# Tile bases on multiples of 256 bytes, side b's filling work held closer to its place, and one addition of the closing norm moved to VectorE

## The chip, the cores and the metric

The kernel runs on one core of one Trainium2 chip. The metric is the device time of one launch in microseconds (us), the median of several runs. Engines are named as in the profile: PE is TensorE (matrix products), PEld its weight loads, DVE is VectorE, ACT ScalarE, POOL GpSimd, SP the engine that issues the DMAs.

## The reference, cut to what matters

One decoder layer on 1024 tokens of width 1024. A layer norm with a modulation from `c` gives `u`; one wide projection of `u` feeds two attention branches and two gates; a last product and a second norm close the layer.

```python
u = _layer_norm(x) * (1.0 + scale) + shift
(q_a, kv_cmp, kv_sel, kv_win, g_nsa, z_a, q_b, kv_b, z_b, g_merge) = _split_columns(u @ w_in)
# branch a: 8 heads; compressed keys, 8 selected blocks of 64 keys, a window of 512
o_a = gts0 * o_cmp + gts1 * o_sel + gts2 * o_win
y_a = o_a * silu(z_a)
# branch b: 8 heads, a window of 128 with a sink logit per head
y_b = _banded_attention(q_b, k_b, v_b, 128, sinks) * silu(z_b)
merged = sigmoid(gm_a) * (y_a @ w_up_a) + sigmoid(gm_b) * (y_b @ w_up_b)
out = merged @ w_out
x = _layer_norm(2 ** 0.25 * x + gate * out) * ln_g + ln_b
```

## The kernel before, in words

Every large product is made of three, to keep float32's precision: an operand is split into a high part (H) and a rest (L), both read as 32-bit "fp32r", and `H*h + H*l + L*h` is summed in PSUM. `load_w` (L239) and `load_w2` (L251) bring a block of weights in by DMA, cut it on ACT (the high part) and on POOL or DVE (the rest), and put both into one tile `whl`.

The stages, in order of time. **Start** (0 to some 140 us): `x` is normed and transposed into `uH` and `uL`, and the first columns of `w_in` are projected. **Attention** (to some 725 us): 32 units, one for each side (a, b), head group and tile of 128 tokens. A unit has three steps: `C` (L742) turns its queries and, on side a, does the compressed branch; `M` (L826) finds each row's maximum; then for each tile of 128 keys `score` (L892) makes two products 512 wide (keys against `qa`, then `qb`), DVE and ACT make `e`, ACT `ph`, POOL `pl`, and `weigh` (L915) multiplies both by the values in 12 short products. **Merge** (to some 850 us): products of `yH`, `yL` with `w_up`. **Close** (to the end): the product with `w_out` in two halves of 512 columns (weights in the pools `wo0` and `wo1`, 8 tiles of tokens each), then `residual` and `norm` (L1424, L1432) for each tile.

Between the attention's products stands *filling* work that depends on nothing there: query projections 256 columns wide (`q_chunk`), and 24 blocks of the gates (`gm_block`, 48 products of 512 columns each), 20 of them inside the attention and 4 after it. `Att.run` deals it out in small steps while it writes the attention down, and a step may not be ordered ahead of an anchor, the last product of an earlier `weigh`:

```python
with L.tc.issue_after(anchors[max(0, len(anchors) - ANCH)]):   # L976, ANCH = 9
    d = fill.step()
```

Within such bounds a scheduler sets the order of each engine's instructions when the program is built; on the chip each engine runs its list in order. Tiles come from pools that lay them one behind another in each partition, so that a tile's first byte depends on the sizes of those before it.

`norm` takes mean and variance of a tile (`mv`, DVE), lets POOL add eps and raise to -0.5 (`rstd`, two POOL instructions at L541 and L542, each on one number per partition), and scales on DVE in two passes, L1441 (needs only `mv`) and L1442 (needs `rstd`).

Of the kernel before, what the change touches and what calls it, by code (L numbers as in the profile page):

```python
# [7 lines left out]
F32 = mybir.dt.float32  # L8
F32R = mybir.dt.float32r
BF = mybir.dt.bfloat16  # L10
F16 = mybir.dt.float16
I32 = mybir.dt.int32
AF = mybir.ActivationFunctionType
OP = mybir.AluOpType
# [4 lines left out]
D = 1024  # L19
S = 1024  # L20
NT = 8
# [4 lines left out]
LN_EPS = 1e-5  # L26
# [7 lines left out]
PARTS = 4  # L34
TRB = (2, 3, 4, 5)
MS, PJ = (2, 3, 4), (6, 7)
ANCH = 9
WARM2 = 1
ADA0 = 3
W0AT = 7  # L40
# [3 lines left out]
TPOOL, TCUT = 0, (256, 256)  # L44
MROW = 1
KEEP = 4
CW = 20
M0 = 0
TAB = 2
# [27 lines left out]
VW = 129  # L77
# [20 lines left out]
class Layer:  # L98
# [32 lines left out]
    def identities(self):  # L131
        nc = self.nc
        ones = self.ones = self.su.tile([128, 128], F32, name="ones")
        nc.gpsimd.memset(ones, 1.0)
        self.idf = self.c.tile([128, 128], F32, name="idf")
        nc.gpsimd.affine_select(self.idf, ones, pattern=[[1, 128]], compare_op=OP.is_equal, fill=0.0, base=0,
                                channel_multiplier=-1)
        self.mhalf = self.c.tile([128, 1], F32, name="mhalf")
        nc.gpsimd.memset(self.mhalf, -0.5)
        self.onec = self.c.tile([128, 1], F32, name="onec")  # L140
        nc.gpsimd.memset(self.onec, 1.0)
        self.poff = self.c.tile([128, 1], F32, name="poff")
        nc.gpsimd.memset(self.poff, POFF)

    def consts(self):
# [93 lines left out]
    def load_w(self, src, k, n, rawp, wp, eng, **place):  # L239

        nc = self.nc
        raw = rawp.tile([128, max(n, 512) if rawp is self.rawp else n], F32, name="raw", tag="raw")[:, :n]
        self.rows_in = nc.sync.dma_start(raw, src(k)).ins
        hl = wp.tile([128, 2, n], F32R, name="whl", **(place or {"tag": "w"}))
        h, l = hl[:, 0, :], hl[:, 1, :]
        self.cast = nc.scalar.copy(h, raw).ins  # L246
        low = eng.tensor_tensor(l, raw, h.bitcast(F32), op=OP.subtract).ins  # L247
        self.low = [self.cast, low, self.low[1]]
        return h, l
# [86 lines left out]
    def start(self):  # L336
        nc, I = self.nc, self.I
        su, c = self.su, self.c
        x = I["x"].rearrange("a (t p) d -> (a t) p d", p=128)
        xt = []  # L340
        wa = I["w_ada"].rearrange("l (k p) c -> (l p) k c", p=128)
        wt, w = {}, {}
# [31 lines left out]
        ps, wps = self.bank(7), self.bank(6)  # L374
# [12 lines left out]
        pf = su.tile([8, 128], F32, name="pos_f")  # L387
        nc.vector.tensor_copy(pf, pi)
        nc.tensor.transpose(ps[:, 24:32], pf, self.idf[:8, :8])
        self.ccol = c.tile([128, 8], F32, name="ccol")  # L390
        bcol = su.tile([128, 16], F32, name="bcol")
        self.pos = su.tile([128, 8], F32, name="pos")
        with self.tc.high_priority(HP):
# [59 lines left out]
        for t in range(NT):  # L453
# [4 lines left out]
            nm, rstd, nb = ln[t]  # L458
# [4 lines left out]
            for hf in range(2):  # L463
                p = trs[t >= 4].tile([128, 4, 128])
# [126 lines left out]
    def new_kv(self, ps, br, vp):  # L591

        self.K[br] = [p.tile([128, 2, 1024], F32R, name=f"K{br}{g}") for g, p in enumerate(ps)]
        self.V[br] = [p.tile([128, NT, VW], F16, name=f"V{br}{g}") for g, p in enumerate(ps)]
        self.new_v(br, vp)

    def new_v(self, br, vp):
# [113 lines left out]
class Att:  # L711


    def __init__(self, L, q, work):

        self.L, self.q, self.w = L, q, work
        self.ms, self.st, self.av = Banks(L, MS), Banks(L, ST), Banks(L, (5,))
        nc = L.nc
        self.nc = nc
        self.U = {}  # L720
        self.qbt = []
        for i in range(2):
            q = work.tile([128, 4, 128], F32R, name=f"qbt{i}")
            nc.gpsimd.tensor_copy(q.rearrange("p h d -> p (h d)"), L.mk[:, 128:129].to_broadcast([128, 512]))
            self.qbt.append(q)
        self.p0 = work.tile([128, 68], F32, name="p0")
        nc.gpsimd.memset(self.p0, 0.0)
        self.n, self.last = 0, []
        self.off = [True, True]
# [9 lines left out]
    def C(self, u):  # L739
        L, nc, w = self.L, self.nc, self.w  # L740
        side, g, qt = u
# [7 lines left out]
                                                       op=OP.subtract)  # L749
# [15 lines left out]
        t = w.tile([128, 4, 64], F32, name="cs", tag="cs")  # L765
        nc.vector.tensor_tensor(t, sc[:, :, 1, :], L.vis[:, qt, None, :].to_broadcast([128, 4, 64]), op=OP.add)
        nc.vector.tensor_tensor(t, t, sc[:, :, 0, :], op=OP.add)
        sm = w.tile([128, 4, 4], F32, name="csm", tag="csm", bufs=2)
        nc.vector.tensor_reduce(sm[:, 0], t, axis=AX.X, op=OP.max)
        (nc.gpsimd if CM else nc.vector).tensor_tensor(t, t, sm[:, 0, :, None].to_broadcast([128, 4, 64]), op=OP.subtract)  # L770
        e = t
# [12 lines left out]
        if qt >= 4:  # L784
            nc.vector.tensor_reduce(self.p0[:, 1:64], pc[:, :, 0:63].rearrange("p h c -> p c h"), axis=AX.X, op=OP.add)
            im = w.tile([128, 4, 16], F32, name="imp", tag="imp")
            nc.vector.tensor_reduce(im[:, 0], self.p0[:, 0:64].rearrange("p (j i) -> p j i", i=4), axis=AX.X, op=OP.add)
            nc.gpsimd.tensor_tensor(im[:, 0], im[:, 0], rawap(self.p0, 4, [[4, 16]]), op=OP.add)
            nc.gpsimd.tensor_tensor(im[:, 1], im[:, 0], L.forced[:, qt], op=OP.add)
            m8 = w.tile([128, 8], F32, name="m8", tag="m8")  # L790
            nc.vector.max(m8, im[:, 1])
            nc.vector.match_replace(im[:, 2], m8, im[:, 1], -3e38)
            sel = st["sel"] = w.tile([128, 16], F32, name="sel", tag="sel", bufs=3)
            nc.vector.tensor_scalar(sel, im[:, 2], -2e38, NEG, op0=OP.is_gt, op1=OP.mult)
            nc.gpsimd.tensor_copy(qbt[:, :, 64:80], sel[:, None, :].to_broadcast([128, 4, 16]))
            self.off[self.n % 2] = False
        else:
            self.rows_off(self.n % 2)
# [25 lines left out]
    def M(self, u):  # L824
        L, nc, w = self.L, self.nc, self.w
        side, g, qt = u  # L826
        st = self.U[u]
        qa, qbt = st["qa"], st["qbt"]
        brs = self.branches(u)
        mx = w.tile([128, 4, 2, 3], F32, name="mx", tag="mx", bufs=2)  # L830
        nc.gpsimd.memset(mx, -3e38)
        if side == "b":

# [1 line left out]
        for bi, (br, kts) in enumerate(brs):  # L835
            n = 128 * len(kts)
# [9 lines left out]
            for a, b, hs in groups:  # L846
                ps = self.ms.tile()
# [107 lines left out]
    def run(self, units, fill, ratio, values):  # L955

        L = self.L
        filled = spent = took = 0.0
        anchors = []
# [6 lines left out]
        def feed(dt):  # L966
            nonlocal filled, spent, took
            took += dt
            if side == "b":
                r = ratio["b"] * max(0.0, fill.time - filled) / max(5.0, need(units) - took)  # L970
            else:
                r = ratio[side]
            spent += dt * r
            while filled < spent:
                if anchors:
                    with L.tc.issue_after(anchors[max(0, len(anchors) - ANCH)]):  # L976
                        d = fill.step()
                elif spent > 6.0:
                    with L.tc.issue_after(self.last[max(0, len(self.last) - 10)]):
                        d = fill.step()  # L980
                else:
                    d = fill.step()
                if d is None:
                    filled = spent
                else:
                    filled += d
# [34 lines left out]
        side = "start"  # L1021
# [14 lines left out]
        for gi, grp in enumerate(groups):  # L1036
            u, bi = steps[grp[0]][:2]
            ui = units.index(u)
            side = "e" if ui < EU else u[0]
            n = ends[ui] - first[u]  # L1040
# [14 lines left out]
            br, fst, lst = steps[grp[0]][2], steps[grp[0]][4], steps[grp[-1]][5]  # L1055
            w = self.weigh(u, br, [(steps[i][3], *emitted.pop(i)) for i in grp], fst, lst, av)
# [62 lines left out]
def run_layer(L):  # L1119
    tc, nc, I = L.tc, L.nc, L.I  # L1120
# [6 lines left out]
    L.uL = pu.tile([128, KT, S], F32R, name="uL")  # L1127
    L.c2, c2_cm = L.pool("const2", side="right")
    L.gts = L.c2.tile([128, NT, 24], F32, name="gts")
    L.sink = L.c2.tile([128, 8], F32, name="sink")  # L1130
    L.kcd = L.c2.tile([128, 2, 2, 64], F32R, name="kcd")
    L.vcb = L.c2.tile([128, 2, 128], F32, name="vcb")
    L.spill = tc.dram_tile([24, 128, S], F32, name="gm_raw")
    L.osp = tc.dram_tile([4, 128, NT, 256], F32, name="o_raw")
    L.pb, pb_cm = L.pool("banks", 1, space=PSUM)
# [11 lines left out]

    wp, w_cm = L.pool("w", 10)
    rp, r_cm = L.pool("wraw", 3)
    L.K, L.V, L.vr, L.vm, L.vinv = {}, {}, {}, {}, {}  # L1150

    flip = [0]
# [150 lines left out]
    ps, yt = Banks(L, (0, 1, 2, 3)), Banks(L, (4, 5, 6))  # L1303
# [32 lines left out]


    pg, pg_cm = L.pool("gateb", side="right")
    gateb = pg.tile([128, D], F32, name="gateb")
    wo0, wo0_cm = L.pool("wo0", 8, side="right")  # L1340
    wor, wor_cm = L.pool("wor", 2, side="right")
    wo = I["w_out"].rearrange("l d c -> (l d) c")
# [28 lines left out]
    for j in range(KT):  # L1371
        ws = []
        for i, nm in enumerate("ab"):
            src = I["w_up_" + nm].rearrange("l (k p) c -> (l p) k c", p=128)
            w = []
# [56 lines left out]
    def norm(t, parts, cuts):  # L1432
        mv = fo.tile([128, 2], F32, name="mv", tag="mv", bufs=2)
        nc.vector.bn_aggr(mv, st[:, t, 0:parts])
        rstd = fo.tile([128, 1], F32, name="rstd", tag="rstd", bufs=3)
        L.rstd(rstd, mv[:, 1:2])
        r = fo.tile([128, D], F32, name="res", tag="res", bufs=2)
        n = D // cuts
        for i in range(cuts):
            c = slice(i * n, i * n + n)  # L1440
            nc.vector.scalar_tensor_tensor(r[:, c], z[:, t, c], mv[:, 0:1], lg[:, c], op0=OP.subtract, op1=OP.mult)  # L1441
            nc.vector.scalar_tensor_tensor(r[:, c], r[:, c], rstd, lb[:, c], op0=OP.mult, op1=OP.add)  # L1442
            nc.sync.dma_start(o[t, :, c], r[:, c])
# [65 lines left out]
```

## Time and profile before

| what | value |
|---|---|
| median of 3 runs | 952.98 us (951.42 to 953.22) |
| the profiled execution's own time | 953.87 us |
| its span, first to last instruction | 952.1 us |
| PE busy | 922.5 us, 97% of the span |
| PEld / DVE / ACT / POOL busy | 83% / 58% / 50% / 61% |
| TensorE clock granted, mean | 0.995 of full speed |

A PE product is pipelined: the profile gives it a start and a modelled end, so what one costs in a dense run is the distance from its start to the next start, not its length. A span has 1.8 us around it that belong to the run's time.

### The profile page before, as it was taken

How to read it: one execution, taken by the hardware profiler on the slowest of the kernel's cores; microseconds unless marked ns; L12 is line 12 of the kernel's file. 1: busy time of each engine (PE TensorE's matmuls, PEld its weight loads, DVE VectorE, ACT ScalarE, POOL GpSimd, SP SyncE). 2: the span in 40 equal slices, each digit the busy share in tenths (PEclk: the TensorE clock that was granted, in tenths of full speed). 3: DMA queues.
4: the chain of work that ended last, by engine and by line, in shares of the span. 5: the costliest groups of instructions: out<-in, count | busy, mean ns of one | idle time of the engine just before them, and what ended most of it. 6: DMA issues, size and time to landing. Idle time of an engine off the chain costs nothing.

```text
span 952.1 us, 18630 instructions
## 1 busy us (share of the span) xinstructions
PE 922.5 (97%) x6592; PEld 785.8 (83%) x6592; DVE 552.8 (58%) x1613; ACT 472.0 (50%) x984; POOL 579.7 (61%) x816
## 2 busy tenths in 40 slices
PE   7899998999999999999999999999989999999995
PEld 5789997788899888898899888889867888778885
DVE  7933356554776553465786643356562675455787
ACT  5846344334555566646554656655763654532100
POOL 7867565355768766767677766765753155635733
PEclk9999999999999999999999999999999999999998
DMA  9914332212202211202201222121303967656222
GB/s 329 287 33 114 82 85 56 78 50 78 67 7 52 61 57 57 62 17 69 73 7 35 73 61 74 46 68 29 92 26 116 379 210 216 189 177 234 83 86 92
DMA packets 93278, 95.40 MB, mean 100 GB/s; under 512 B 7616, under 2 KB 72192, under 8 KB 93184
## 3 DMA queue, kind: packets, MB, share of 16 engines
q1 hardware_dynamic: 93184, 94.21, 31.9%
q8 instruction: 52, 0.85, 0.4%
q14 instruction: 42, 0.34, 0.1%
HBM read 73.21 MB, written 20.97 MB: 99 GB/s over the span
## 4 chain that ended last, share of the span: by engine, by line
PE 85%; DVE 6%; ACT 3%; POOL 2%; DMA 2%; issue 1%; SPq 0%; POOLq 0%; DVEq 0%; ACTq 0%
PE bank L107 82%; POOL rstd L541 1%; DVE res L1442 1%; DVE jk L873 1%; PE bank L885 1%; PE bank L754 1%; DMA wada<-in_w_ada_dram 1%; ACT lnT L471 1%; PE bank L1321 1%; DVE stats L1430 1%; DVE z L1429 1%; DVE e L902 1%; DVE gt L1428 0%; DMA raw<-in_w_in_dram 0%; ACT lnT L445 0%
## 5 line engine op out<-in xcount | busy, mean ns | idle before, releaser
L107 PE MATMUL bank<-whl,uH 128*128 128x256 f32 (+3 forms) x1168 | 271.6, 323 | 2.8 <-ACT uH L448 2.4
L107 PE MATMUL bank<-uH,whl 128*128 128x512 f32 x768 | 249.9, 400 | 0.2
L912 POOL TENSOR_TENSOR pl<-e,ph 128x512 f16<-128x512 f32 x162 | 188.2, 1167 | 72.2 <-ACT ph L909 58.5
L107 PEld LDWEIGHTS bank<-whl,uH 128*128 128x128 f32 x1168 | 197.7, 189 | 21.5 <-ACT uH L448 3.5
L107 PE MATMUL bank<-whl,uL 128*128 128x256 f32 (+3 forms) x584 | 181.6, 319 | 0.0
L107 PEld LDWEIGHTS bank<-uH,whl 128*128 128x128 f32 x768 | 142.6, 189 | 29.6 <-PE bank L885 0.4
L107 PE MATMUL bank<-uL,whl 128*128 128x512 f32 x384 | 152.0, 396 | 0.0
L258 POOL TENSOR_TENSOR whl<-raw,whl 128x256 fp32r<-128x256 f32 x128 | 100.5, 791 | 80.1 <-ACT whl L257 72.1
L107 PEld LDWEIGHTS bank<-whl,uL 128*128 128x128 f32 x584 | 109.5, 188 | 8.0
L909 ACT CAST ph<-e 128x512 f16<-128x512 f32 x162 | 98.2, 618 | 29.3 <-PE bank L107 27.5
L873 DVE CUSTOM_DVE_ANT_0 jk<-bank,mk 128x256 bf16<-128x256 f32 (+3 forms) x168 | 74.0, 441 | 34.2 <-PE bank L107 29.6
L906 ACT ACTIVATE e<-bank,poff 128x512 f32<-128x512 f32 x92 | 62.0, 687 | 54.4 <-PE bank L107 51.1
L107 PEld LDWEIGHTS bank<-uL,whl 128*128 128x128 f32 x384 | 72.4, 189 | 15.9
L257 ACT CAST whl<-raw 128x256 fp32r<-128x256 f32 x128 | 50.7, 403 | 62.4 <-PE bank L107 39.2
L107 PE MATMUL bank<-yH,whl 128*128 128x512 f32 x256 | 80.6, 398 | 0.0
L902 DVE TENSOR_TENSOR e<-bank,mkt 128x512 f32<-128x512 f32 x70 | 47.7, 689 | 45.1 <-PE bank L107 42.4
L107 PEld LDWEIGHTS <-pl 128*128 128x128 f16 x648 | 59.3, 98 | 16.0 <-issue 10.3
L247 POOL TENSOR_TENSOR whl<-raw,whl 128x256 fp32r<-128x256 f32 (+3 forms) x60 | 53.5, 897 | 23.7 <-ACT whl L246 21.4
L904 ACT ACTIVATE e<-e,poff 128x512 f32<-128x512 f32 x70 | 50.0, 722 | 35.2 <-DVE e L902 34.9
L107 PEld LDWEIGHTS <-ph 128*128 128x128 f16 x1296 | 64.9, 97 | 0.8 <-issue 0.3
L246 ACT CAST whl<-raw 128x256 fp32r<-128x256 f32 (+3 forms) x72 | 34.4, 482 | 58.9 <-DMA raw<-in_w_out_dram 32.7
L107 PEld LDWEIGHTS bank<-yH,whl 128*128 128x128 f32 x256 | 47.9, 188 | 11.7 <-issue 0.5
(292 smaller groups left out, 1732.9 us busy)
## 6 DMA issues: line engine op xcount, KB each, us to landing
raw<-in_w_in_dram SPq DMA_DIRECT2D x136, 128.0 KB, 2.2
gm_raw<-gmo SPq DMA_DIRECT2D x48, 256.0 KB, 2.1
wada<-in_w_ada_dram SPq DMA_DIRECT2D x16, 512.0 KB, 6.2
sg<-gm_raw SPq DMA_DIRECT2D x32, 256.0 KB, 3.3
x<-in_x_dram SPq DMA_DIRECT2D x8, 512.0 KB, 5.3
o_raw<-q SPq DMA_DIRECT2D x32, 128.0 KB, 1.9
o<-o_raw SPq DMA_DIRECT2D x8, 512.0 KB, 6.2
z<-gm_raw SPq DMA_DIRECT2D x16, 256.0 KB, 6.5
```

The source lines that it names most:

```text
L107: return self.nc.tensor.matmul(out, l, r, start=start, stop=stop, skip_group_check=True)
L246: self.cast = nc.scalar.copy(h, raw).ins
L247: low = eng.tensor_tensor(l, raw, h.bitcast(F32), op=OP.subtract).ins
L257: nc.scalar.copy(hl[:, 0], raw)
L258: eng.tensor_tensor(hl[:, 1], raw, hl.bitcast(F32)[:, 0], op=OP.subtract)
L471: nc.scalar.copy(dst, p)
L873: nc.vector.tensor_tensor_reduce(o, src, m, 1.0, -3e38, OP.add, OP.max, mx[:, h, g if side == "b" else bi, slots[h]:slots[h] + 1])
L902: nc.vector.tensor_tensor(e.rearrange("p (h q) -> p h q", h=4), ps.rearrange("p (h q) -> p h q", h=4), L.mkt[:, int(edge), None, :].to_bro ...
L904: nc.scalar.activation(e, e, AF.Exp, bias=L.poff)
L906: nc.scalar.activation(e, ps, AF.Exp, bias=L.poff)
L909: nc.scalar.copy(ph, e)
L912: eng.tensor_tensor(pl, e, ph, op=OP.subtract)
```

## The change

Padding and a new order of allocation move tiles, so that nearly all that TensorE reads begins at a multiple of 256 bytes in its partition. From the built programs, first byte of the tile modulo 256:

| tile | read by PE as | before | after |
|---|---|---|---|
| `uH`, `uL` | both operands | 0 | 0 |
| `whl` of the filling and of the merge | either operand | 0, 64, 128, 192 in turn | 0 |
| `whl` in `wo0` / in `wo1` | moving | 224 / 0 | 0 / 0 |
| `yH`, `yL` | moving | 96 | 0 |
| `qa` / `qb` | both / moving | 160 / 224 | 0 |
| keys `K` | both | 96, 128, 160, 192 | 0 |
| `ph`, `pl` | stationary | 224 | 0 |
| values `V` | moving | 96, 128, 160, 192 | 0, 128 |

No product is added or taken away, and none changes its shape. Side b's filling steps may now stand behind the anchor two back (`ANCHB` = 2) in place of nine. In `norm` DVE adds eps; POOL keeps the power.

```diff
-ANCH = 9
+ANCH, ANCHB = 9, 2
...
+        room = -(-n // 64) * 64
...
-        hl = wp.tile([128, 2, n], F32R, name="whl", **(place or {"tag": "w"}))
-        h, l = hl[:, 0, :], hl[:, 1, :]
+        hl = wp.tile([128, 2, room], F32R, name="whl", **(place or {"tag": "w"}))
+        h, l = hl[:, 0, :n], hl[:, 1, :n]
...
-        self.V[br] = [p.tile([128, NT, VW], F16, name=f"V{br}{g}") for g, p in enumerate(ps)]
+        if len(self.K) == 2:
+            for x in self.K:
+
+                self.V[x] = [p.tile([128, 1088], F16, name=f"V{x}{g}") for g, p in enumerate(ps)]
+                self.V[x] = [v[:, :NT * VW].rearrange("p (t c) -> p t c", c=VW) for v in self.V[x]]
...
-        self.p0 = work.tile([128, 68], F32, name="p0")
+        self.p0 = work.tile([128, 128], F32, name="p0")[:, :68]
...
-        mx = w.tile([128, 4, 2, 3], F32, name="mx", tag="mx", bufs=2)
+        mx = w.tile([128, 4, 8], F32, name="mx", tag="mx", bufs=2)[:, :, :6].rearrange("p h (b c) -> p h b c", c=3)
...
-                    with L.tc.issue_after(anchors[max(0, len(anchors) - ANCH)]):
+                    with L.tc.issue_after(anchors[max(0, len(anchors) - (ANCHB if side == "b" else ANCH))]):
...
+    rp.tile([128, 8], F32, name="pad", bufs=1)
...
-    gateb = pg.tile([128, D], F32, name="gateb")
+    gateb = pg.tile([128, D + GPAD], F32, name="gateb")[:, :D]
...
-        L.rstd(rstd, mv[:, 1:2])
+
+        nc.vector.tensor_scalar(rstd, mv[:, 1:2], LN_EPS, None, op0=OP.add)
+        nc.gpsimd.tensor_tensor(rstd, rstd, L.mhalf, op=OP.pow)
```

Left out are five more tiles padded or allocated in another order (`csm`, `m8`, `sink`, `ccol` and the small constants).

Up to the last units of side a (PE's first 4470 products) every engine's order is what it was. From there it differs. PE where side b begins, before (names: `Kw`, `Ks` keys; `uH,whl` and `uL,whl` filling; `qbt`, `qat` turning queries):

```order
L107 MATMUL bank_8951<-qb,Kw_936 128x512
L107 MATMUL bank_9105<-uH,whl 128x512
L107 MATMUL bank_9105<-uL,whl 128x512
L107 MATMUL bank_9105<-uH,whl 128x512 x2
L107 MATMUL bank_9010<-qa,Kw_936 128x512
L107 MATMUL bank_9010<-qb,Kw_936 128x512
L107 MATMUL bank_9105<-uL,whl 128x512
L885 MATMUL bank_9156<-idr,qbt_1881 128x128 x4
L107 MATMUL bank_9105<-uH,whl 128x512 x2
L107 MATMUL bank_9105<-uL,whl 128x512
L754 MATMUL bank_9180<-idr,qat 128x128 x4
```

The same place after:

```order
L108 MATMUL bank_8952<-qb,Kw_935 128x512
L108 MATMUL bank_9106<-uH,whl 128x512
L108 MATMUL bank_9106<-uL,whl 128x512
L890 MATMUL bank_9157<-idr,qbt_1882 128x128 x2
L108 MATMUL bank_9011<-qa,Kw_935 128x512
L108 MATMUL bank_9011<-qb,Kw_935 128x512
L890 MATMUL bank_9157<-idr,qbt_1882 128x128 x2
L759 MATMUL bank_9181<-idr,qat 128x128 x4
```

Two filling products stand there in place of eight; the five steps from here on, up to the next filling run of nine, have none between their scores.

PE late in side b, where the filling had been used up, before (one unit's scores and the next unit's maxima):

```order
L107 MATMUL bank_10569<-qa,Kw_935 128x512
L107 MATMUL bank_10612<-qa,Kw_935 128x512
L107 MATMUL bank_10628<-Kw_935,qa 128x256 x2
L885 MATMUL bank_10562<-idr,qbt_1883 128x128 x4
L107 MATMUL bank_10569<-qb,Kw_935 128x512
L107 MATMUL bank_10612<-qb,Kw_935 128x512
L107 MATMUL bank_10635<-Kw_935,qa 128x256 x2
```

The end of the same unit and the start of the next, after:

```order
L108 MATMUL bank_10613<-qb,Kw_934 128x512
L108 MATMUL bank_10535<-uH,whl 128x512 x2
L108 MATMUL bank_10535<-uL,whl 128x512
L108 MATMUL bank_10636<-Kw_934,qa 128x256 x2
L108 MATMUL bank_10535<-uH,whl 128x512 x2
L108 MATMUL bank_10535<-uL,whl 128x512
L108 MATMUL bank_10535<-uH,whl 128x512 x2
L108 MATMUL bank_10535<-uL,whl 128x512
L759 MATMUL bank_10690<-idr,qat 128x128 x4
L108 MATMUL bank_10677<-qa,Kw_934 128x512
L108 MATMUL bank_10714<-qa,Kw_934 128x512
L890 MATMUL bank_10670<-idr,qbt_1882 128x128 x4
```

Nine filling products have come into a stretch that had none.

DVE in the last `norm`, before:

```order
L1434 BN_AGGR mv<-stats 128x2
L1441 SCALAR_TENSOR_TENSOR res<-z,mv,lg 128x512 x2
L1442 SCALAR_TENSOR_TENSOR res<-res,rstd,lb 128x512 x2
```

And after:

```order
L1440 BN_AGGR mv<-stats 128x2
L1443 TENSOR_SCALAR rstd<-mv 128x1
L1449 SCALAR_TENSOR_TENSOR res<-z,mv,lg 128x512 x2
L1450 SCALAR_TENSOR_TENSOR res<-res,rstd,lb 128x512 x2
```

The addition stands ahead of the first pass in all eight tiles, and POOL's list loses its eight instructions of L541 there.

## Rows read from the trace of the kernel before

**Rows 1.** The chain of work that ended last, shares by engine, from the page.
```profile
PE 85%; DVE 6%; ACT 3%; POOL 2%; DMA 2%; issue 1%; SPq 0%; POOLq 0%; DVEq 0%; ACTq 0%
```
**Rows 2.** Windows: stretch, its length, busy and count of PE, PEld, DVE, ACT, POOL.
```profile
675.00:725.00 50.00, 44.66 (x381) 35.64 (x378) 28.74 (x106) 34.82 (x72) 29.51 (x45) 1.00 0.17 49
```
**Rows 3.** Timeline of PE (start, length, instruction), close, first half (`wo0`).
```profile
868.32 0.40 PE L107 MATMUL bank<-whl,uL 128*128 128x512 f32 x1
...
870.42 0.40 PE L107 MATMUL bank<-whl,uL 128*128 128x512 f32 x1
```
**Rows 4.** Timeline of PE, close, second half (`wo1`).
```profile
911.33 0.39 PE L107 MATMUL bank<-whl,uL 128*128 128x512 f32 x1
...
913.37 0.39 PE L107 MATMUL bank<-whl,uL 128*128 128x512 f32 x1
```
**Rows 5.** Timeline of PE, filling between two steps of side b.
```profile
717.59 0.62 PE L107 MATMUL bank<-uH,whl 128*128 128x512 f32 x2
...
718.96 0.62 PE L107 MATMUL bank<-uH,whl 128*128 128x512 f32 x2
...
721.04 0.63 PE L107 MATMUL bank<-uH,whl 128*128 128x512 f32 x2
```
**Rows 6.** Timeline of PE, the first six of another filling block, on aligned tiles.
```profile
534.81 0.62 PE L107 MATMUL bank<-uH,whl 128*128 128x512 f32 x2
...
536.20 0.20 PE L107 MATMUL bank<-Vs,pl 128*128 128x65 f16 x1
```
**Rows 7.** Timeline of PE, merge.
```profile
800.43 0.63 PE L107 MATMUL bank<-yH,whl 128*128 128x512 f32 x2
...
801.83 0.63 PE L107 MATMUL bank<-yH,whl 128*128 128x512 f32 x2
```
**Rows 8.** Timeline of PE, products 256 wide: query projection, not aligned.
```profile
138.66 0.40 PE L107 MATMUL bank<-whl,uH 128*128 128x256 f32 x2
...
139.72 0.40 PE L107 MATMUL bank<-whl,uH 128*128 128x256 f32 x2
```
**Rows 9.** Timeline of PE, products 256 wide: last tile of the close, aligned.
```profile
939.27 0.40 PE L107 MATMUL bank<-whl,uH 128*128 128x256 f32 x2
...
941.43 0.40 PE L107 MATMUL bank<-whl,uH 128*128 128x256 f32 x2
```
**Rows 10.** Timeline of PE, `qb` products of two units late in side b.
```profile
694.60 0.70 PE L107 MATMUL bank<-qb,Kw 128*128 128x512 f32 x2
...
698.75 0.73 PE L107 MATMUL bank<-qb,Kw 128*128 128x512 f32 x2 [0.67 <-ACT qb L887]
```
**Rows 11.** ACT's groups from 675 to 720 us: busy, mean ns, idle before.
```profile
L904 ACT ACTIVATE e<-e,poff 128x512 f32<-128x512 f32 x17 | 12.0, 720 | 10.1 <-DVE e L902 9.9
L909 ACT CAST ph<-e 128x512 f16<-128x512 f32 x16 | 9.7, 616 | 0.2
```
**Rows 12.** Timeline of DVE, second pass of `norm`, two tiles in a row.
```profile
930.72 1.28 DVE L1442 SCALAR_TENSOR_TENSOR res<-res,rstd,lb 128x1024 f32<-128x1024 f32 x1 [0.76 <-POOL rstd L542]
...
936.37 1.28 DVE L1442 SCALAR_TENSOR_TENSOR res<-res,rstd,lb 128x1024 f32<-128x1024 f32 x1 [0.75 <-POOL rstd L542]
```
**Rows 13.** Timeline of POOL, eps in the second of these tiles.
```profile
934.39 1.31 POOL L541 TENSOR_SCALAR rstd<-mv 128x1 f32<-128x1 f32 x1 [3.71 <-DVE mv L1434]
```
**Rows 14.** The same POOL instruction in the start stage, shortest/median/longest ns.
```profile
L541 POOL TENSOR_SCALAR lnv<-lnv x8: 211/223/677, 6.3 to 24.6; 128x1 f32<-128x1 f32 x8
```
**Rows 15.** Groups of DVE: an operation on one number per partition.
```profile
L326 DVE TENSOR_SCALAR vmxs<-vmxs 128x1 f32<-128x1 f32 x1 | 0.2, 156 | 0.0
```
**Rows 16.** Timeline of all engines, the last `norm`.
```profile
945.42 1.42 DVE L1441 SCALAR_TENSOR_TENSOR res<-z,mv,lg 128x512 f32<-128x512 f32 x2
945.47 0.77 POOL L541 TENSOR_SCALAR rstd<-mv 128x1 f32<-128x1 f32 x1 [3.47 <-DVE mv L1434]
946.33 0.92 POOL L542 TENSOR_TENSOR rstd<-rstd,mhalf 128x1 f32<-128x1 f32 x1
947.28 1.42 DVE L1442 SCALAR_TENSOR_TENSOR res<-res,rstd,lb 128x512 f32<-128x512 f32 x2 [0.45 <-POOL rstd L542]
```

More of the change, by code (lines that the diff above doesn't have):

```diff
@@ L46 @@
 KEEP = 4
+GPAD = 56
 CW = 20
@@ L134, in identities @@
         nc.gpsimd.memset(ones, 1.0)
+        self.mhalf, self.onec, self.poff = (self.c.tile([128, 1], F32, name=n) for n in ("mhalf", "onec", "poff"))
+        self.ccol = self.c.tile([128, 8], F32, name="ccol")
         self.idf = self.c.tile([128, 128], F32, name="idf")
@@ L137, in identities @@
                                 channel_multiplier=-1)
-        self.mhalf = self.c.tile([128, 1], F32, name="mhalf")
         nc.gpsimd.memset(self.mhalf, -0.5)
-        self.onec = self.c.tile([128, 1], F32, name="onec")
         nc.gpsimd.memset(self.onec, 1.0)
-        self.poff = self.c.tile([128, 1], F32, name="poff")
         nc.gpsimd.memset(self.poff, POFF)
@@ L389, in start @@
         nc.tensor.transpose(ps[:, 24:32], pf, self.idf[:8, :8])
-        self.ccol = c.tile([128, 8], F32, name="ccol")
         bcol = su.tile([128, 16], F32, name="bcol")
@@ L767, in C @@
         nc.vector.tensor_tensor(t, t, sc[:, :, 0, :], op=OP.add)
-        sm = w.tile([128, 4, 4], F32, name="csm", tag="csm", bufs=2)
+        sm = w.tile([128, 4, 8], F32, name="csm", tag="csm", bufs=2)[:, :, :4]
         nc.vector.tensor_reduce(sm[:, 0], t, axis=AX.X, op=OP.max)
@@ L789, in C @@
             nc.gpsimd.tensor_tensor(im[:, 1], im[:, 0], L.forced[:, qt], op=OP.add)
-            m8 = w.tile([128, 8], F32, name="m8", tag="m8")
+            m8 = w.tile([128, 40], F32, name="m8", tag="m8")[:, :8]
             nc.vector.max(m8, im[:, 1])
@@ L1129, in run_layer @@
     L.gts = L.c2.tile([128, NT, 24], F32, name="gts")
-    L.sink = L.c2.tile([128, 8], F32, name="sink")
     L.kcd = L.c2.tile([128, 2, 2, 64], F32R, name="kcd")
     L.vcb = L.c2.tile([128, 2, 128], F32, name="vcb")
+    L.sink = L.c2.tile([128, 32], F32, name="sink")[:, :8]
     L.spill = tc.dram_tile([24, 128, S], F32, name="gm_raw")
```

## The prediction

> **What bounds the kernel now.** I read the chain of waits first: 85% of the span's chain runs over PE [rows 1], so what shortens a product of PE in a dense run shortens the program, save where PE waits for others. Those places come from the windows of 50 us. Late in side b PE is busy 44.66 of 50.00 us [rows 2], so 5.3 us go unused there, and in the close the timeline of DVE shows that its gaps are waits for POOL [rows 12]. Then I looked at PE's timeline for the pitch of its products, since a busy share of 97% hides it: a product that takes 233 ns where 227 would do is busy all the same.
>
> The pitch is where the trace speaks plainest. The two halves of the close do the same products with the same operands. They differ in the pool of their weights, whose tiles begin at 224 modulo 256 in `wo0` and at 0 in `wo1`. Nine products take 2.10 us in the first (870.42 − 868.32) and 2.04 in the second [rows 3, 4]: 233.3 against 226.7 ns each, 6.7 ns or 2.9%. That the tile's first byte decides it is my reading, since nothing else that I can see differs. The same comparison is less clean in the filling. Within one stretch six products on aligned tiles take 1.37 us, 228.3 each, and the nine behind them, on tiles at 192 and 128, take 2.08, 231.1 each [rows 5]; but six others, aligned too, take 1.39, 231.7 each [rows 6]. The merge, where `yH` lies at 96, has six in 1.40, 233.3 [rows 7].
>
> **The change, part by part.** The sum is made against the profiled execution's own 953.87 us (its span of 952.1 and 1.8 around it), which is 0.9 above the median of 952.98. Counts are from the loops.
>
> Alignment, dense products 512 wide:
> - `wo0`, 8 tiles of tokens × 8 weights × 3 = 192 products, 6.7 ns each by [rows 3, 4]: 1.3 us, and these rows leave it little room.
> - Filling, 24 blocks of 48 = 1152. If aligned tiles go as in [rows 6], at 231.7, they lose 0.6 ns each, 0.7 us in all; if they reach the 226.7 of [rows 4], they gain 4.4 ns, 5.1 us. I take [rows 5]'s own difference, 2.8 ns, since it is the same work side by side: 3.2 us. Most of it stands in the attention, where PE is the chain.
> - Merge, 8 × 2 × 2 × 12 = 384 products: from 233.3 to 228.3, 1.9 us; ends 0.6 (at 231.7) and 2.5 (at 226.7).
> - Scores, 162 steps of two: `qa`, `qb` and the keys all come to 0. No row shows such products in a dense run; the filling's 2.8 ns on 324 makes 0.9, of which I take 0.8, with ends −0.2 and 1.4 from the filling's ends.
> - Products 256 wide speak against the change. Nine in the query projection, not aligned, take 1.06 us, 117.8 each [rows 8], while 18 aligned ones take 2.16, 120.0 each [rows 9]. With 960 query products that would be a loss of 2.1 us. But [rows 9] stand in a stage with another partner, and two rows are few; I take a loss of 1.0, with ends −2.1 and 0.
>
> That makes 1.3 + 3.2 + 1.9 + 0.8 − 1.0 = 6.2 us. Part of it falls where PE waits for others, in the start and late in side b; I strike 0.5 and keep 5.7. Padding itself issues nothing: no DMA, no product. POOL's one fill of `mx` grows from 24 numbers per partition to the same 24 in a wider tile, which costs nothing that I can see.
>
> On this point the Trainium skill states a rule, in "SBUF — State Buffer", "Specifications (TRN2)": SBUF is read in lines of 16 bytes, each crossing has its price, and at least two reads of a line are wanted for full speed. All bases before are multiples of 32 bytes, so every operand already begins on such a line, and by this rule the alignment gives nothing. [Rows 3, 4] disagree: 233.3 against 226.7 ns with nothing but the base between them.
>
> Filling of side b: the anchor two back in place of nine doesn't shorten any work; it moves filling from early in side b to late. Before, the filling is used up some 14 score steps (seven units) ahead of the end, and there PE goes at ACT's pace: two units' `qb` products stand 4.15 us apart, and the later ones wait 0.67 us for ACT's `qb` [rows 10], while ACT has an `e` of 720 and a `ph` of 616 ns per step and the query's copies besides [rows 11]. The 5.3 us that PE misses in [rows 2] over 14 steps are 0.38 us a step. After, the order shows five score steps without filling at the seam from side a to b, and some three at the end. At the same 0.38 these cost 1.9 + 1.1 = 3.0, so 2.3 are won; I take 2.0, since a unit with few filling products is only half covered. Ends: all 5.3 won, or, if a dozen steps are left bare and each waits the 0.67 of [rows 10], 8.0 lost in place of 5.3, which is −2.7. A filling product may stand close behind a `weigh` now; that `weigh` waits for POOL's `pl`, and everything behind it in PE's list, the filling too, waits with it. What covered that wait before was filling that stood ahead of it. No DMA is issued elsewhere by more than these steps: a filling step brings its own weights and writes its own block, at 0.17 of the DMA engines [rows 2].
>
> Eps on DVE: in the close a tile's second pass follows 5.65 us behind the last one's (936.37 − 930.72), and DVE waits 0.75 for POOL's `rstd` in each [rows 12]. PE's 24 products of a tile take 24 × 226.7 = 5.44 us, so DVE sets the pace, by 0.2 only. POOL's eps takes 1.31 us there [rows 13], though the same instruction takes 0.211 in the start stage [rows 14]; it lies beside DVE's first pass. After, DVE adds eps itself, ahead of that pass. The nearest row for one number per partition is 156 ns [rows 15]. POOL's power then starts as soon as DVE's add is done, which is about the first pass's start. If it is stretched as eps was, it ends near 0.4 us behind that pass: in the last `norm` the power began at 946.33, halfway through the pass that ended at 946.84, and ended 0.41 after it, so that the gap was 0.45 [rows 16]. The gap then falls from 0.75 to 0.45 and the add takes 0.16 of it: 0.14 a tile, 7 × 0.14 = 1.0 for the tiles in a row, of which PE's floor of 5.44 takes nothing yet, and nothing to speak of for the last one, whose gap is 0.45 already. I take 1.0. If the power isn't stretched at all the gap goes, 0.6 a tile, until PE's floor stops it at 0.2 a tile, 1.5 plus 0.3 at the end: 1.8. If the power waits for the whole pass and takes its 0.92 then, the gap grows by 0.17 and the add comes on top: 0.33 × 8 = 2.6 lost. The first gap is nearer to what [rows 13, 16] show.
>
> The Trainium skill's rule on this, "SBUF — State Buffer", "SBUF: two separate sides", is that VectorE and GpSimd share a port pair, which one of them locks for a whole instruction. The 1.31 against 0.211 us agrees with it. By a strict lock the power, queued behind a pass that began first, would end its whole length after the pass, and the sum would be the loss above.
>
> Sum: 5.7 + 2.0 + 1.0 = 8.7 us, 945.2 on the profiled execution's scale and 944.3 on the median's.
>
> **Rivals.** All times are on the median's scale.
> - *Alignment gives nothing beyond `wo0`.* The filling behaves as in [rows 6], and what [rows 5] show is chance. For it: those 231.7 on aligned tiles. Against it: the merge's 233.3, as high as `wo0`'s. 1.3 + 2.0 + 1.0 = 4.3: 948.7. The skill's rule on lines of 16 bytes leads close to here; without `wo0` it is 950.0.
> - *All dense products come to 226.7.* The slow ones of [rows 6] would come from one operand off its base somewhere, which is gone when every one is aligned. 1.3 + 5.1 + 2.5 + 1.4 − 0.5 = 9.8, with 3.0 from the other two parts 12.8: 940.2. For it speak [rows 4]; against it [rows 6].
> - *Slower: the near anchor makes filling wait with `weigh`.* Place: PE's list in side b, 32 score steps. If each waits 0.67 us [rows 10] for `pl` with the filling queued behind it, PE misses 21.4 in place of 5.3, 16.1 more; less the 6.7 of the other two parts it is 9.4 slower: 962.4. It decides from 12.0 us more, 0.38 a step. For it: the filling no longer runs ahead. Against it: POOL is busy only 29.51 of 50 us there [rows 2], so `pl` should be in time.
> - *The gain is taken by other engines.* PE's shorter products only lengthen its waits for ACT and POOL. Against it: 85% of the chain is PE's [rows 1]. Some 2 us are left: 951.0.
>
> **How the numbers follow.** My forecast has 0.55, alignment beyond `wo0` worth nothing 0.15, all at 226.7 0.17, slower 0.06, taken by others 0.07. The forecast's own range is 940 to 948.5, from the filling's and side b's ends taken partly together; with the two nearest rivals and part of the fourth it is 937.5 to 950.5, and about 2 in 10 lie outside. 0.2%, 1.9 us, is about what can be told from no change. Faster by more: nearly all of the forecast and of the two alignment rivals, and half of the last, 0.88. Slower by more: 0.06 and a remainder from side b's and the power's losing ends together, 0.07. The same: 0.05.
>
> **What would show it.** `wo0`: three products in 0.68 us in place of 0.70, and the merge's six in 1.37 in place of 1.40. Filling: six in 1.37 throughout; if many stand at 1.39 the first rival holds, at 1.36 the second. Side b: PE misses under 3 us in its last 50, with new waits for ACT at the seam, near 600 us; if waits for `pl` come at most steps, the slow rival holds. Close: the gap ahead of the second pass near 0.45 and the cycle near 5.5; a gap near 0.9 is the strict lock. The forecast as a whole is wrong if the time is above 951.1 or below 937.5.

## The result, and the profile after

The changed kernel takes 945.46 us (944.77 to 946.25, 6 runs) against 952.98: a ratio of 0.9925, interval 0.9915 to 0.9936. The forecast of 944.3 was 1.2 us too low and its range held the time. Its profiled execution has a span of 943.5 us, 8.6 below before's. Where these 8.6 come from is read off the start of the same product in both traces (us from the span's start; both issue 6592 products, and the order is the same up to side b; the first product of the merge stands four places later in after's list, so that some 0.3 us of the merge's 2.54 belongs to the order):

| place | before | after | lead gained in the stretch up to it |
|---|---|---|---|
| attention begins (850th product) | 153.21 | 152.47 | 0.74 |
| 1200th product | 216.06 | 213.52 | 1.80 |
| 4470th product, where the orders part | 595.20 | 590.74 | 1.92 |
| merge | 759.84 | 757.03 | −1.65 |
| `wo0` | 852.76 | 847.41 | 2.54 |
| `wo1` | 897.95 | 891.37 | 1.23 |
| last product | 941.67 | 935.09 | 0.00 |
| end of span | 952.13 | 943.54 | 2.01 |

The chain of waits (the page of after), to be set beside [rows 1]:

```profile
PE 69%; DMA 8%; DVE 8%; POOL 7%; ACT 3%; issue 3%; SPq 1%; DVEq 0%; POOLq 0%; ACTq 0%
```

PE's share falls from 85% to 69% and loads take 8%, yet PE is busy 125.00 of the 125 us from 725 to 850 in both traces. Where two paths end within a few tenths, the chain changes sides; it doesn't say that PE now waits. But in the close the path has changed. After, DVE begins its tiles straight behind its cut of the last `wo1` block, which waits for ACT's (the first fence); before, it still waits for PE's product behind that cut (the second):

```profile
894.54 0.69 DVE L249 TENSOR_TENSOR whl<-raw,whl 128x512 fp32r<-128x512 f32 x1 [2.39 <-ACT whl L248]
```
```profile
903.60 0.69 DVE L1428 TENSOR_TENSOR gt<-bank,gateb 128x512 f32<-128x512 f32 x1 [0.75 <-PE bank L107]
```

In nine of the fourteen traces of this case DVE has no wait for PE there, and its first second pass follows that cut by 6.95 us (7.20 with eps on POOL). In those the end hangs on when these weights are ready, and not on PE.

Timeline of PE after, in `wo0`, then in the merge: nine products take 2.04 us, 226.7 ns each, where [rows 3] have 2.10; six take 1.36, 226.7 each, where [rows 7] have 1.40.

```profile
863.27 0.39 PE L108 MATMUL bank<-whl,uL 128*128 128x512 f32 x1
...
865.31 0.39 PE L108 MATMUL bank<-whl,uL 128*128 128x512 f32 x1
```
```profile
797.09 0.62 PE L108 MATMUL bank<-yH,whl 128*128 128x512 f32 x2
...
798.45 0.62 PE L108 MATMUL bank<-yH,whl 128*128 128x512 f32 x2
```

The filling shows what [rows 5, 6] left open. This is the same run of 19 products in both traces, first after, then before:

```profile
456.03 0.40 PE L108 MATMUL bank<-uL,whl 128*128 128x512 f32 x1
...
458.10 0.39 PE L108 MATMUL bank<-uL,whl 128*128 128x512 f32 x1
...
460.14 0.40 PE L108 MATMUL bank<-uL,whl 128*128 128x512 f32 x1
```
```profile
459.91 0.40 PE L107 MATMUL bank<-uL,whl 128*128 128x512 f32 x1
...
462.00 0.39 PE L107 MATMUL bank<-uL,whl 128*128 128x512 f32 x1
...
464.08 0.39 PE L107 MATMUL bank<-uL,whl 128*128 128x512 f32 x1
```

After, the first nine take 2.07 us (230 ns each), the next nine 2.04 (226.7). Before, they take 2.09 and 2.08. An aligned run begins uneven and comes to 226.7 within some nine products; before, each block of six brings a new base, and no run comes to rest. Over all runs of filling from 200 us to the merge, some 1000 products (distances above 260 ns, which hold waits, left out), the mean at each place of a run stays near 232 ns before; after, it is 230.5 at the first, 228.2 at the seventh and 226.7 from the eleventh on. Over all of them it falls from 231.9 to 228.7. [Rows 6] are aligned, but the first products of their run. The score products 512 wide, which stand in short groups, don't gain: 232.0 before, 231.8 after.

Late in side b after, the window answers [rows 2], and PE's timeline shows why its clock reads 0.93:

```profile
675.00:725.00 50.00, 46.98 (x342) 38.63 (x341) 21.89 (x77) 26.29 (x55) 26.04 (x39) 0.93 0.22 61
```
```profile
681.92 0.50 PE L108 MATMUL bank<-Kw,qa 128*128 128x256 f32 x2 [1.55 <-ACT qa L761]
...
683.69 0.72 PE L759 MATMUL bank<-idr,qat 128*128 128x128 f32 x4 [0.97 <-DVE mx L878]
...
686.31 1.20 PE L108 MATMUL bank<-uH,whl 128*128 128x512 f32 x2
...
690.85 0.70 PE L108 MATMUL bank<-uH,whl 128*128 128x512 f32 x2
```

PE misses 3.0 us in place of 5.3 here. Ahead of this window, from 600 to 675 us, before misses nothing, but after misses 2.2, 1.5 of them up to 650 (before, then after):

```profile
600.00:650.00 50.00, 50.00 (x465) 43.71 (x464) 24.35 (x82) 29.62 (x60) 30.38 (x45) 1.00 0.19 57
```
```profile
600.00:650.00 50.00, 48.49 (x462) 41.94 (x461) 27.24 (x97) 32.42 (x70) 33.63 (x50) 1.00 0.18 54
```

In the whole of side b PE misses 5.2 us in place of 5.3: the waits have been moved, not removed. And behind two of them the granted clock falls to its lower level, 0.5, until some 690 us: a pair of products has 1.20 where it has 0.70 later. By the clock of 0.93, 3.5 us of the 50 are lost. Before has such a stretch too, from 191 to 195 us, in which the clock loses 1.7 us; after has none there, and that is most of the 1.80 in the table.

In the close, DVE's second passes (the first fence) stand 5.41 us apart where [rows 12] have 5.65; the gap is 0.44, and the last tile's second pass, at 938.72, has none (compare [rows 16]). POOL's power (the second) takes 1.45 us beside DVE's pass; before, where DVE waits for it, it takes 0.56 (the third).

```profile
923.13 1.28 DVE L1450 SCALAR_TENSOR_TENSOR res<-res,rstd,lb 128x1024 f32<-128x1024 f32 x1 [0.44 <-POOL rstd L1444]
...
928.54 1.28 DVE L1450 SCALAR_TENSOR_TENSOR res<-res,rstd,lb 128x1024 f32<-128x1024 f32 x1 [0.44 <-POOL rstd L1444]
```
```profile
927.05 1.45 POOL L1444 TENSOR_TENSOR rstd<-rstd,mhalf 128x1 f32<-128x1 f32 x1 [3.95 <-DVE rstd L1443]
```
```profile
935.78 0.56 POOL L542 TENSOR_TENSOR rstd<-rstd,mhalf 128x1 f32<-128x1 f32 x1
```

### The profile page after: what moved, and what is told of

Its sections match the earlier page's. It is cut to its first block, busy times and chain, and to the rows that moved or that the text cites. A ratio compares the mean times of both kernels' runs of the same rounds, so it can differ in the third digit from the quotient of the medians.

```text
span 943.5 us, 18610 instructions
## 1 busy us (share of the span) xinstructions
PE 914.3 (97%) x6592; PEld 787.0 (83%) x6592; DVE 550.2 (58%) x1621; ACT 471.4 (50%) x984; POOL 575.6 (61%) x808
## 4 chain that ended last, share of the span: by engine, by line
PE 69%; DMA 8%; DVE 8%; POOL 7%; ACT 3%; issue 3%; SPq 1%; DVEq 0%; POOLq 0%; ACTq 0%
PE bank L108 65%; DMA sg<-gm_raw 2%; POOL z L1421 2%; DMA raw<-in_w_ada_dram 2%; DMA raw<-in_w_out_dram 1%; DMA raw<-in_w_in_dram 1%; POOL rstd L1444 1%; DVE res L1450 1%; POOL pl L917 1%; PE bank L890 1%; DVE jk L878 1%; DMA x<-in_x_dram 1%; PE bank L759 1%; POOL whl L260 1%; PE bank L1327 1%
```

## The experiments

Times scatter by 1.5 to 6.5 us between runs of one kernel, so each timed verdict is a ratio to runs of before on the same chip, and the traces are compared by stretches.

**Near filling undone, twice.** `ANCH, ANCHB = 9, 9` in the changed kernel.

> The changed kernel with side b's filling behind the anchor nine back again (ANCHB = 9). Theory A, from the two traces set side by side product by product: from the start of side b to the merge the lead of the changed kernel falls from 4.5 to 2.8 us, and PE's granted clock is 0.5 from 685 to 690 us right behind two waits of 1.55 and 0.97 us; so the near filling costs some 2 to 3 us, and this kernel takes 942 to 944 us, with no stretch at half clock late in side b. Theory B, the prediction's: the near filling wins 2.0 us, so this kernel is slower than the changed one, 947.5 us.

947.07 us, ratio 0.9941 (0.9926 to 0.9957).

> The changed kernel with ANCHB = 9 once more. Theory C: the near filling gives 0.9 us at full clock and loses 1.7 to 3.4 us by the half clock that it brings, so this kernel takes no longer than the changed one, 944 to 945.5 us. Rival, the prediction's: the near filling is worth something, and this kernel is 1 to 2 us slower than the changed one again, as the first time (947.07 against 945.46).

944.89, 0.9911 (0.9898 to 0.9924). The two lie on either side of the changed kernel's 0.9925 and 0.9918: the near filling is worth nothing that these runs can tell. The first run alone would have spoken for the prediction.

**Alignment alone, twice.** The same with `L.rstd(rstd, mv[:, 1:2])` back in `norm`.

> The kernel before with the padding and the order of allocation alone (ANCHB = 9, eps on POOL as before). Theory A: products give 2.2 us in the attention up to side b and about 0.9 in it, 2.5 in the merge and 1.2 in wo0, 0.5 before the attention, and the half clock at 191 us, 1.7 us, goes if it hangs on the alignment: 944.0, or 945.7 if the clock falls here too. Theory B, the prediction's: 5.7 us, 947.3. Rival (alignment gives wo0's 1.3 alone): 951.7.

948.68, 0.9960 (0.9945 to 0.9975).

> The alignment alone once more. The first time it took 3.8 us less than before (ratio 0.9960), while its trace's stretches at full clock add up to some 6.2 us (1.9 from 216 us to side b, 0.9 in b, 2.2 in the merge, 1.2 in wo0). If stretches at half clock and late weights by chance made up the difference, this trace's full-clock stretches give the same four numbers, and the times pooled with the first lie between; if something steady is lost, it stands in the same place of both traces.

947.09, 0.9935 (0.9920 to 0.9950). Together some 0.9948, 5.0 us. Both traces give 1.92 and 1.93 us from the 1200th product to side b, 2.22 and 2.23 in the merge, 1.23 and 1.23 in `wo0`. Side b gains 0.87 in the first trace with the near filling undone, at full clock, but only 0.04 and 0.01 in these two, which both have a half clock there. In the close something is lost, too, but not steadily. In the second trace the lead is 6.57 us at the start of `wo0`, 7.80 at that of `wo1` and 6.50 at the end, since DVE begins its tiles behind the last `wo1` block there, not behind PE, and then keeps its 5.66 us a tile: its cut of that block starts at 894.59, after 2.00 of waiting for ACT's, and its second passes stand at 930.12 and 935.79. In the first, 0.8 of `wo0`'s 1.23 comes through to the end.

**Eps alone.** In the kernel before, the two lines of the diff in `norm`.

> The kernel before with eps added on DVE in the last norm and nothing else. Theory A, by the trace after: a tile's second pass follows 5.41 us behind the last one's in place of 5.65, and the last tile loses its gap of 0.45: 7 x 0.24 + some 0.3 = 2.0 us, 951.0. Theory B, the prediction's: 0.14 a tile, 1.0 us in all, 952.0. By a strict lock (the power runs wholly behind the first pass): slower, 955.6.

951.95, 0.9993 (0.9983 to 1.0002): 0.7 us, not clear of noise, and at most 1.6 by the interval. Its trace has the mechanism as the changed kernel's: gaps of 0.44 us and cycles of 5.40 (second passes at 928.87 and 934.27). From the last product to the end it takes 8.55 us where before takes 10.46: 1.91 less. Why the times show less than that isn't known. On aligned kernels the ratios go from a mean of 0.9948 to 0.9926, about 2 us, but the two runs of either kernel differ by 0.0025 and 0.0030.

**Near filling alone, twice.** In the kernel before, `ANCHB` = 2 for side b.

> The kernel before with side b's filling behind the anchor two back and nothing else. Theory A: 2 to 3 us slower than before, 955 to 956, with a stretch at half clock late in side b. Theory B, the prediction's: 2.0 faster, 951.0. If the half clock of the changed kernel has nothing to do with the filling's place, it is absent here.

953.18, 1.0003 (0.9990 to 1.0016). Neither theory: nothing gained or lost in time. In its trace side b is 0.89 us shorter, at full clock, and the merge 0.3; PE misses 4.8 us in side b in place of 5.3, 2.2 of them ahead of 675 us.

> The kernel before with the near filling alone, once more, for a second trace. It orders side b as the changed kernel does, but its first trace had no half clock there. Theory C as it stands (the nearly bare steps bring the half clock) expects it here between 685 and 700 us, 1.7 to 3.4 us long; if it is absent again, the bare steps alone don't bring it: the shorter aligned products ahead of them, or the time between, have a part in it.

A single run, 953.41. This time the half clock is there, and side b is 1.13 us longer than before's. The windows of the two traces, first and second:

```profile
675.00:725.00 50.00, 47.39 (x379) 39.08 (x378) 23.32 (x83) 27.93 (x61) 28.55 (x43) 1.00 0.25 68
```
```profile
675.00:725.00 50.00, 46.87 (x350) 38.62 (x350) 22.79 (x80) 28.50 (x61) 29.17 (x46) 0.97 0.25 67
```

The same program falls in one execution and not in another. PE is *busier* than before's 44.66 in both: a fall hides in the busy time.

**Other anchors, and the changed kernel again.** `ANCHB` = 4 (twice) and 3.

> The changed kernel with side b's filling behind the anchor four back (ANCHB = 4): two score steps without filling at the seam in place of four, and none of the nearly bare steps late in side b (the changed kernel's ones ahead of 684 us have 0, 1 and 0 filling products in a row). Theory C: such a bare stretch is where PE waits, and the half clock behind it costs 3.4 us in the changed kernel's trace; here neither comes late in side b, and the time is 942 to 943.5 us. Rival: the half clock late in side b comes by chance, whatever the filling, or the place of the filling is worth nothing: 945.5, like the changed kernel.

944.75, 0.9901 (0.9886 to 0.9917).

> The changed kernel once more, unchanged, for a second trace and for times beside the other runs of this call. Theory C: the half clock late in side b comes again behind the same two waits, between 680 and 692 us. Rival (chance): it is absent, or stands elsewhere, and this trace's span is some 3 us shorter than 943.5.

946.07, 0.9918 (0.9902 to 0.9934). The half clock came again behind the same two waits, but at half its length: side b is 0.39 us shorter than before's, not 1.65 longer.

> ANCHB = 4 once more, for a second trace and more times. Theory C: no half clock from 650 to 725 us, and again about 1 us less than the changed kernel: a ratio to before near 0.990. Rival: the first lead of 1.3 us was chance, and the ratio is near the changed kernel's 0.992; then the half clock may stand late in side b as well.

946.56, 0.9920 (0.9908 to 0.9932).

> The changed kernel with side b's filling behind the anchor three back (ANCHB = 3): three bare score steps at the seam, none but every second step from there to the end. Theory C (nearly bare steps in a row late in side b bring the half clock): no half clock from 650 to 725 us, side b some 1 us shorter than before's order gives it, and a time 1 to 2 us under the changed kernel's (944 to 945). Rival: like the changed kernel, 945.5 to 946, with the half clock late in side b again.

947.11, 0.9926 (0.9912 to 0.9940), with the half clock from 716 us, where theory C had none. With four, neither trace has it: the granted clock is 1.00 from 675 to 725 us in both. Both traces give side b some 1.07 us less than before. Whether four beats two isn't settled: 1.3 us in one set, none against the ratios of the other. No version here clearly beats the changed kernel.

**Bases.** In the changed kernel `GPAD` = 24 and `wo1.tile([128, 16], F32, name="pad", bufs=1)` ahead of the weights of `wo1`.

> The changed kernel with the weights of wo0 at 128 modulo 256 and those of wo1 at 64. If multiples of 256 are what counts, both halves of the close take 233 ns a product in place of 226.7 and the time rises by 1.2 us in each half that PE sets; if multiples of 64 or 128 do, the one or both stay at 226.7. By lines of 16 bytes: 226.7 in both.

One run, 946.09. PE's timeline in `wo0`, then in `wo1`:

```profile
864.34 0.40 PE L108 MATMUL bank<-whl,uL 128*128 128x512 f32 x1
...
866.44 0.39 PE L108 MATMUL bank<-whl,uL 128*128 128x512 f32 x1
```
```profile
908.82 0.39 PE L108 MATMUL bank<-whl,uL 128*128 128x512 f32 x1
...
910.88 0.39 PE L108 MATMUL bank<-whl,uL 128*128 128x512 f32 x1
```

At 128 nine products take 2.10 us, 233.3 ns each, as at 224 [rows 3]; at 64 they take 2.06, 228.9, and not the expected 233. `wo0`'s lead of 1.23 us is gone. The reading of [rows 3, 4] is now shown: of all that PE reads there the base alone was moved, and of the four bases seen (0, 64, 128, 224) only 0 gives 226.7.

## Why the prediction was right, and where it wasn't

- *Alignment, 5.7 us.* Right in cause and size; the terms are off both ways. `wo0` gave 1.23 for 1.3. The merge gave 2.2 in most aligned traces for 1.9; its products go to some 227, the upper end. From the 1200th product to side b it is 1.9, in side b 0.87 (the first trace with the near filling undone, at full clock). These four make 6.2. Timed alone it is 5.0, since late half clocks and the weights of `wo1` took part of it. In the filling I took [rows 5, 6] for two possible pitches; they are the settled and the unsettled part of an aligned run. The mean over all of it falls by 3.2 ns, near the 2.8 that I chose; that is luck, since the lengths of the runs set it. The scores' 0.8 was wrong: 0.2 ns on 324 products is 0.1 us. By the Trainium skill's lines of 16 bytes ("SBUF — State Buffer", "Specifications (TRN2)") 64, 128 and 224 would be as good as 0; the measured 228.9, 233.3 and 233.3 ns against 226.7 decide against that reading. The second rival, 940.2 from all products at 226.7, fails by the unsettled starts.
- *Products 256 wide, a loss of 1.0.* No run isolates it. In runs of such products the trace has mostly 120 ns after, as in [rows 9], and mostly 118 before; the mean goes from 121.3 to 121.9 with the alignment alone, which on 960 products is a loss of 0.6.
- *Filling of side b, 2.0.* Wrong, and in two steps. I priced every bare step at 0.38 us. The five at the seam cost 2.2 for 1.9, which is near; the three at the end cost 2.6 for 1.1 (near filling alone, at full clock), so PE missed 4.8 in all where I had 3.0. At full clock side b gained only 0.89 and the merge 0.3. And I held the clock fixed: it falls there in four of the five traces with this order, which takes the gain back. The rival that filling would wait behind `weigh` at most steps didn't come true: two waits of 0.5 are for `pl`, and the long ones for ACT's `qa` and DVE's `mx`, at the bare steps.
- *Eps, 1.0.* The mechanism and the gap (0.45 foreseen, 0.44 found) were right, the size was half of what came: 2.0 in the traces. The add costs 0.07 us ahead of the pass, not 0.16, since the pass starts (921.42) before the add's 0.15 from 921.35 are over. And the last tile loses its whole gap: its power, 0.92 long, starts with the first of two passes and is done before them. The Trainium skill's exclusive lock ("SBUF — State Buffer", "SBUF: two separate sides") agrees in that the power is stretched, 1.45 beside one pass of 1024 and 0.92 beside the first of two of 512 against 0.56 by itself. In both it ends 0.40 behind the pass beside which it began, most of its 0.56, though not the whole length that a strict queue would give. I had priced that rival with the stretched 0.92, and so much too high.

So the total was right partly by luck. By the traces alignment and eps came out some 1.5 above their forecast, and side b's 2.0 was largely lost. By the times alignment gave 5.0, eps about 2 on aligned kernels (0.7 alone) and the near filling nothing that shows, 7 of the 7.5 us measured.

Theory C, that the nearly bare steps of the near filling bring the half clock, fell as stated. Late in side b it is in four of five traces of `ANCHB` = 2 and in the one of 3, but also in three of the four aligned ones of 9; it is absent in two of 9 unaligned and two of 4. Waits of PE stand ahead of it in every case that I read, but what decides between two executions of one program stays open. Nor is it excluded that the alignment has a part: seven of the ten aligned traces have it and one of the four others, too few to tell. That a steady stream through the bare steps would keep the clock up wasn't tried.

## What to carry to other kernels

Where two stages do the same products, compare their pitch before anything else; if it differs, look at the tiles' first bytes, and give whatever TensorE streams or loads a multiple of 256. The gain comes in long dense runs; short groups of products kept their pitch here. Where filling is moved, count the waits over the whole stretch, at the place that it leaves too. A wait of PE removed is worth its length only if the clock behind it stays as it is: read the granted clock of the stretch beside the busy time. And a faster PE hands on what it saves only as long as the next stage waits for PE: from `wo0` to the end alignment alone gained −0.07 or 0.8 us and eps alone 1.91; the seven traces with both gained 1.5 to 3.3, so that these traces don't show whether the two help each other.

## What the runs showed of the hardware

- The pitch of a product 512 wide in a dense run: 226.7 ns with the moving tile at 0 modulo 256, 228.9 at 64, 233.3 at 128 and at 224. With only the stationary side off (the filling before) a long run stays near 232 and doesn't settle; aligned, it settles at 226.7 within about ten products. Products 256 wide take a median of 118 ns before and 120 aligned.
- In the attention the granted clock falls to its lower level, 0.5, for 3.4 us (6.8 in two of the traces), behind waits of PE wherever I read what came ahead of it, and in some executions of a program and not in others: between 150 and 200 us in five of the fourteen traces, whatever the kernel. By the clock 3.4 us at this level lose 1.7. What side b lost by them was 0.85 in the aligned kernels with nine, whose gain there is 0.87 without and 0.01 to 0.04 with one, and 2.0 with the near filling alone (0.89 against −1.13). Against an effect of 7.5 us two of them more or less are nearly half.
